# An mLSTM layer in fp32 on one core: five instead of four of eight chunks of the input projection by seven products

## The chip, the core and the metric

The program runs on one core of a Trainium2 chip. TensorE (PE) multiplies, VectorE (DVE), ScalarE (ACT) and GpSimd (POOL) work elementwise, SyncE (SP) issues DMAs. Each engine runs its own instructions in the order of the program and waits on semaphores for the others. The metric is the device time of one execution in microseconds; the kernel before has a median of 1795.51 us in three runs (1791.73 to 1797.22).

## The reference

One decoder layer of depth 1, so only the mLSTM mixer is computed, on 256 tokens of width 4096 in fp32, with 8 heads (query and key width 256, value width 512):

```python
h = rms_norm(x, norm_w)
u = h @ w_in                          # 4096 x 16400 columns
qk, v, og, z, ig, fg = split(u)
qk = silu(causal_dwconv(qk, conv_w, conv_b))      # 4 taps
# per head, in two chunks of 128 tokens:
a   = exp(decay - max) * (q @ k.T)                # causal
hc  = (a @ v + inter-chunk part) / max(|sum|, exp(-max))
hn  = hc * rsqrt(mean(hc * hc) + EPS) * out_norm_w
y   = hn * sigmoid(og) * silu(z)
out = x + y @ w_out                   # 4096 x 4096
```

## The kernel before

**Products.** Each fp32 operand is split into a high part (`hi`, rounded to the type fp32r) and the rest (`lo`). A product is three matmuls: hi by hi, hi by lo, lo by hi (`matmul3`, L138). The activations are the stationary side and stay in SBUF for a whole projection; the weights stream through as the moving side, 512 columns a matmul. `split` (L133) makes the two parts: ACT writes `hi` with a copy (L135), DVE writes `lo = src - hi` (L136). `operand` (L144) does this for a weight block of 128x1024, which is one buffer of the four `whi` and one of the four `wlo`; the raw block lies in one of six `wraw` buffers, loaded by SP with 512 KB a transfer (L157). All three kinds have the size of 1056 floats (RAW), 4224 bytes, so that the starts of neighbouring buffers differ by 33 times 128 bytes.

**Pairs and chunks.** The first phase projects head 0's q, k, v and the gates with plain products. Then 15 pairs of column blocks of `w_in` follow, 2 x 512 columns each: for head h first `qkv` (q and k; v), then `oz` (the output gate; z); head 0 has `oz` only. Four pairs of `w_out` (`o0` to `o3`) end the kernel. In `project_pair` (L317) the 4096 rows are 8 chunks of 512. A chunk in `FAST` (0, 2, 4, 6) is done by seven products of half blocks instead of eight (the Strassen-Winograd form): `STEPS` (L45) lists its loads, its four sums of weight blocks on DVE (`add`, L281) and its seven uses, named P1 to P7 after the PSUM bank they add into. Each use is one `operand` and 6 matmuls. A plain chunk is four uses of 12 matmuls each, without sums. The uses of a fast chunk form four groups, (P1), (P5, P3), (P7, P6, P2) and (P4), and after each group one use of a plain chunk follows.

**The rest of a head.** After a pair, `combine` (L349) reads the seven banks. What follows is put in a queue of small closures, of which `pump` runs some after every use: the four convolution taps of q and k (`taps`, L443) and their SiLU (`silu`, L451), the decay matrix, q k, row sums, values and a reciprocal root (`head`, L462, with `rsqrt`, L121), the gates (`gate_1`, L639), then `finish` and `turn`, which transposes y and writes it to DRAM (`spill`, by POOL). `build` (L196) makes the stationary operands of a chunk, `build_x` (L241) those of x after scaling. The order on each engine is fixed when the program is built.

**Names.** `w_qkv` is a raw block, `wh_qkv` and `wl_qkv` its parts, `..._P` those of a fast use; `w_qkv3_2_21` is head 3, chunk 2, block 21. `acc` and `pt` belong to the convolution, `sg` to the gate, `rs_...` and `ss` to the reciprocal root.

Of the kernel before, what the change touches and what calls it, by code (L numbers as in the profile page):

```python
# [716 lines left out]
```

## Time and profile before

| | us |
|---|---|
| median of 3 runs | 1795.51 |
| the profiled execution, its own time | 1793.31 |
| its span, first to last instruction | 1791.6 |
| PE busy | 1756.1 (98%) |
| DVE busy | 1655.5 (92%) |
| ACT busy | 1107.1 (62%) |

The profiled execution's time is 1.7 us over its span and 2.2 us under the median. A matmul or a DVE instruction is recorded longer than the distance to the next, since neighbours overlap in the pipeline; the distance between two starts is what an instruction costs when the engine has no gap. "Busy" counts overlapping time once.

### The profile page before, as it was taken

The page shows a single profiled execution, that of the slowest core. Times are in us where ns is not written, and L with a number is a line of the kernel's source. Part 1 is how long each engine was busy: PE and PEld are TensorE (multiplying, and loading weights), DVE is VectorE, ACT ScalarE, POOL GpSimd, SP SyncE. Part 2 cuts the span into 40 slices and gives each one's busy share as a digit, 9 for nine tenths or more (in the row PEclk, how much of TensorE's full clock was granted, in tenths as well). Part 3 has the DMA queues.
Part 4 walks back from the last instruction along what each step waited for, and adds up shares of the span by engine and source line. Part 5 has one row for each costly group of instructions (what it writes and reads, how often), then busy time and mean ns, then how long its engine had stood idle before and what let it go on. Part 6 is the DMA issues. An engine that isn't in the chain of part 4 may idle for free.

```text
span 1791.6 us, 21695 instructions
## 1 busy us (share of the span) xinstructions
PE 1756.1 (98%) x7804; PEld 1419.5 (79%) x7804; DVE 1655.5 (92%) x1823; ACT 1107.1 (62%) x1271; POOL 12.1 (1%) x29
## 2 busy tenths in 40 slices
PE   9979999999999999999999999999999989999998
PEld 8867878888888788788878887888788768787876
DVE  5899999999999999989998999899999999989897
ACT  7566666665666666656666566566656666565654
POOL 0000000000000000000000000000000000000000
PEclk9999999999999999999999999999999989999999
DMA  9755565556555656565556566655555747767563
GB/s 368 262 167 193 171 221 191 193 190 219 192 192 179 217 182 202 174 234 188 188 192 218 188 193 205 208 186 195 202 193 183 234 154 258 244 212 241 195 221 121
DMA packets 107724, 365.67 MB, mean 204 GB/s; under 512 B 12128, under 2 KB 12512, under 8 KB 107616
## 3 DMA queue, kind: packets, MB, share of 16 engines
q1 hardware_dynamic: 105360, 356.95, 59.4%
q0 software_dynamic: 1968, 6.82, 1.0%
q8 instruction: 61, 1.00, 0.2%
q10 hardware_dynamic: 288, 0.52, 0.1%
q14 instruction: 47, 0.39, 0.1%
HBM read 356.38 MB, written 7.86 MB: 203 GB/s over the span
## 4 chain that ended last, share of the span: by engine, by line
PE 86%; DVE 7%; ACT 3%; issue 2%; DMA 1%; SPq 0%; DVEq 0%; ACTq 0%
PE P_oz L140 11%; PE P_oz L141 11%; PE P_oz L142 11%; PE P_qkv L141 10%; PE P_qkv L142 10%; PE P_qkv L140 10%; PE P_o L141 5%; PE P_o L142 5%; PE P_o L140 5%; ACT wh_qkv_P L135 1%; PE first_P L140 1%; PE first_P L141 1%; PE first_P L142 1%; DVE wl_oz_P L136 1%; DVE wl_oz L136 1%
## 5 line engine op out<-in xcount | busy, mean ns | idle before, releaser
L135 ACT ACTIVATE wh_oz_P<-w_oz 128x1024 fp32r<-128x1024 f32 x224 | 233.8, 1056 | 166.2 <-DVE w_oz L281 85.7
L136 DVE TENSOR_TENSOR wl_oz_P<-w_oz,wh_oz_P 128x1024 fp32r<-128x1024 f32 x224 | 269.0, 1216 | 19.5 <-ACT wh_oz_P L135 19.5
L135 ACT ACTIVATE wh_qkv_P<-w_qkv 128x1024 fp32r<-128x1024 f32 x196 | 206.4, 1060 | 114.3 <-PE P_qkv L142 77.6
L136 DVE TENSOR_TENSOR wl_qkv_P<-w_qkv,wh_qkv_P 128x1024 fp32r<-128x1024 f32 x196 | 236.8, 1220 | 29.8 <-ACT wh_qkv_P L135 28.7
L141 PE MATMUL P_oz<-wl_oz,lhs_x 128*128 128x512 f32 x512 | 202.7, 396 | 0.0
L142 PE MATMUL P_oz<-wh_oz,lhs_x 128*128 128x512 f32 x512 | 201.3, 393 | 0.0
L140 PE MATMUL P_oz<-wh_oz,lhs_x 128*128 128x512 f32 x512 | 195.2, 396 | 1.8 <-ACT wh_oz L135 0.9
L141 PE MATMUL P_oz<-wl_oz_P,lhs_x 128*128 128x512 f32 x448 | 179.0, 400 | 1.1 <-DVE wl_oz_P L136 1.1
L140 PE MATMUL P_oz<-wh_oz_P,lhs_x 128*128 128x512 f32 x448 | 175.9, 402 | 3.9 <-ACT wh_oz_P L135 3.8
L141 PE MATMUL P_qkv<-wl_qkv,lhs_x 128*128 128x512 f32 x448 | 177.4, 396 | 0.9 <-DVE wl_qkv L136 0.9
L142 PE MATMUL P_oz<-wh_oz_P,lhs_x 128*128 128x512 f32 x448 | 177.1, 395 | 0.0
L142 PE MATMUL P_qkv<-wh_qkv,lhs_x 128*128 128x512 f32 x448 | 176.1, 393 | 0.0
L135 ACT ACTIVATE wh_o_P<-w_o 128x1024 fp32r<-128x1024 f32 x112 | 117.6, 1059 | 93.5 <-PE P_o L142 53.1
L135 ACT ACTIVATE wh_qkv<-w_qkv 128x1024 fp32r<-128x1024 f32 x112 | 118.5, 1058 | 79.2 <-PE P_qkv L142 66.0
L140 PE MATMUL P_qkv<-wh_qkv,lhs_x 128*128 128x512 f32 x448 | 166.7, 393 | 0.0
L135 ACT ACTIVATE wh_oz<-w_oz 128x1024 fp32r<-128x1024 f32 x128 | 134.8, 1053 | 47.4 <-PE P_oz L142 22.5
L136 DVE TENSOR_TENSOR wl_oz<-w_oz,wh_oz 128x1024 fp32r<-128x1024 f32 x128 | 155.7, 1217 | 7.5 <-ACT wh_oz L135 7.3
L281 DVE TENSOR_TENSOR w_oz<-w_oz,w_oz 128x1024 f32<-128x1024 f32 x128 | 155.7, 1217 | 0.5
L141 PE MATMUL P_qkv<-wl_qkv_P,lhs_x 128*128 128x512 f32 x392 | 154.7, 395 | 0.0
L142 PE MATMUL P_qkv<-wh_qkv_P,lhs_x 128*128 128x512 f32 x392 | 154.2, 393 | 0.0
L136 DVE TENSOR_TENSOR wl_o_P<-w_o,wh_o_P 128x1024 fp32r<-128x1024 f32 x112 | 135.3, 1219 | 18.9 <-ACT wh_o_P L135 18.8
L140 PE MATMUL P_qkv<-wh_qkv_P,lhs_x 128*128 128x512 f32 x392 | 150.2, 398 | 1.1 <-ACT wh_qkv_P L135 1.0
(216 smaller groups left out, 3436.7 us busy)
## 6 DMA issues: line engine op xcount, KB each, us to landing
w_oz<-in_w_in SPq DMA_DIRECT2D x256, 512.0 KB, 4.3
w_qkv<-in_w_in SPq DMA_DIRECT2D x224, 512.0 KB, 4.3
w_o<-in_w_out SPq DMA_DIRECT2D x128, 512.0 KB, 4.4
wf<-in_w_first SPq DMA_DIRECT2D x15, 528.0 KB, 6.7
wf<-in_w_first SPq DMA_DIRECT2D x15, 512.0 KB, 6.7
xr<-in_x SPq DMA_DIRECT2D x8, 512.0 KB, 8.6
xn<-in_xT SPq DMA_DIRECT2D x8, 512.0 KB, 5.7
xo<-in_x SPq DMA_DIRECT2D x16, 256.0 KB, 5.2
```

The costliest lines, as they stand in the source:

```text
L135: nc.scalar.activation(hi, src, AF.Copy)
L136: nc.vector.tensor_sub(lo, src, hi.bitcast(F32))
L140: nc.tensor.matmul(ps, a[0], b[0], start=first, stop=False)
L141: nc.tensor.matmul(ps, a[0], b[1], start=False, stop=False)
L142: nc.tensor.matmul(ps, a[1], b[0], start=False, stop=last)
L281: nc.vector.tensor_add(raw[step[1]], raw[step[1]], raw[step[2]])
```

## The change

Chunk 1 of `w_in` joins the fast chunks, so that a pair of `w_in` has five fast and three plain chunks; `w_out` keeps four and four. The plain uses are spread evenly over the 20 groups, so that 8 of the 20 have none behind them. `whi` and `wlo` shrink to 1024 floats (4096 bytes), and all eight buffers then start at the same place modulo 4096 bytes; the wide blocks of the first phase go through two pairs of other buffers. Some DVE work becomes other work: a tap is two ACT copies and one DVE addition for both halves, SiLU is ACT's own function in place of a sigmoid and a DVE product, `build_x` scales by the norm's weights on ACT, and ten of the twelve small steps of the reciprocal root of a head go to POOL, in another form of 13 steps there. The DMA scratch shrinks to 2048 bytes.

```diff
-FAST = (0, 2, 4, 6)
+FAST = {"x": (0, 1, 2, 4, 6), "y": (0, 2, 4, 6)}
...
-    def rsqrt(dst, src, n, tag):
+    def rsqrt(dst, src, n, tag, eng=nc.vector):
...
         nc.vector.tensor_scalar(r.bitcast(I32), i, -1.0, float(0x5F3759DF), op0=OP.mult, op1=OP.add)
         for it in range(3):
-            nc.vector.tensor_mul(t, r, r)
-            nc.vector.scalar_tensor_tensor(t, t, -0.5, src, op0=OP.mult, op1=OP.mult)
-            nc.vector.scalar_tensor_tensor(dst if it == 2 else r, t, 1.5, r, op0=OP.add, op1=OP.mult)
+            eng.tensor_mul(t, r, r)
+            eng.tensor_mul(t, t, src)
+            eng.tensor_scalar(t, t, -0.5, 1.5, op0=OP.mult, op1=OP.add)
+            eng.tensor_mul(dst if it == 2 else r, t, r)
...
-        hi = wpool.tile([P, RAW], F32R, name=f"wh_{name}", tag="whi")[:, :n]
-        lo = wpool.tile([P, RAW], F32R, name=f"wl_{name}", tag="wlo")[:, :n]
+        hi = wpool.tile([P, HK * NB], F32R, name=f"wh_{name}", tag="whi")[:, :n]
+        lo = wpool.tile([P, HK * NB], F32R, name=f"wl_{name}", tag="wlo")[:, :n]
         split(hi, lo, src)
         return hi, lo
 
+    def wide_operand(name, src, n):
+
+        tags = (("v0", "v1"), ("cA", "cB"))[n % 2]
+        hi, lo = (work.tile([P, RAW], F32R, name=f"w{i}_{name}", tag=tag)[:, :src.shape[-1]]
+                  for i, tag in enumerate(tags))
+        split(hi, lo, src)
+        return hi, lo
...
-        def scaled(j0):
-            def run():
-                if j0 == 0:
-                    nc.sync.dma_start(src, xT[:, c * CK:(c + 1) * CK, :])
-                for j in range(j0, j0 + 2):
-                    k = c * CK + j
-                    nc.vector.scalar_tensor_tensor(src[:, j, :], src[:, j, :], nw[:, k:k + 1], rstdB,
-                                                   op0=OP.mult, op1=OP.mult)
+        def scaled():
+            nc.sync.dma_start(src, xT[:, c * CK:(c + 1) * CK, :])
+            for j in range(CK):
+                nc.scalar.activation(src[:, j, :], src[:, j, :], AF.Copy, scale=nw[:, c * CK + j:c * CK + j + 1])
+            nc.vector.tensor_mul(src, src, rstdB.unsqueeze(1).to_broadcast([P, CK, T]))
...
-        for c in FAST:
-            for group in fast_steps(name, w, off, c):
-                steps += group
-                if plain:
-                    steps.append(plain.pop(0))
+        for i, group in enumerate(groups):
+            steps += group + plain[i * len(plain) // len(groups):(i + 1) * len(plain) // len(groups)]
...
-            def taps(a):
+            def tap(j):
                 def run():
-                    acc, pt, ct = t_["acc"], t_["pt"], ct0 + a
-                    for j in range(1, CONV):
-                        nc.vector.scalar_tensor_tensor(acc[:, a, j:], pt[:, a, :T - j], cw[:, 3 - j, ct:ct + 1],
-                                                       acc[:, a, j:], op0=OP.mult, op1=OP.add)
+                    acc, tp, pt = t_["acc"], t_["tp"], t_["pt"]
+                    for a in range(2):
+                        nc.scalar.activation(tp[:, a, :T - j], pt[:, a, :T - j], AF.Copy,
+                                             scale=cw[:, 3 - j, ct0 + a:ct0 + a + 1])
+                    nc.vector.tensor_add(acc[:, :, j:], acc[:, :, j:], tp[:, :, :T - j])
                 return run
 
             def silu():
-                nc.scalar.activation(t_["sg"], t_["acc"], AF.Sigmoid)
-                nc.vector.tensor_mul(t_["acc"], t_["acc"], t_["sg"])
+                nc.scalar.activation(t_["acc"], t_["acc"], AF.Silu)
...
-            nc.vector.tensor_scalar(ss, ss, 1.0 / DV, EPS, op0=OP.mult, op1=OP.add)
-            rsqrt(s2, ss, NT, f"h{h}")
+            nc.gpsimd.tensor_scalar(ss, ss, 1.0 / DV, EPS, op0=OP.mult, op1=OP.add)
+            rsqrt(s2, ss, NT, f"h{h}", nc.gpsimd)
...
-                sg[0] = big("sg", [P, NT, NB])
                 nc.scalar.activation(A, A, AF.Sigmoid)
-                nc.scalar.activation(sg[0], B, AF.Sigmoid)
+                nc.scalar.activation(B, B, AF.Silu)
 
-            todo += [gate_1, lambda B=B, sg=sg: nc.vector.tensor_mul(B, B, sg[0]),
-                     lambda A=A, B=B: nc.vector.tensor_mul(B, B, A)]
+            todo += [gate_1, lambda A=A, B=B: nc.vector.tensor_mul(B, B, A)]
...
-    nc = bacc.Bacc("TRN2", target_bir_lowering=False, num_devices=1, dynamic_dma_scratch_size=4096)
+    nc = bacc.Bacc("TRN2", target_bir_lowering=False, num_devices=1, dynamic_dma_scratch_size=2048)
```

The first place to look at is DVE in the pair `qkv3` at chunk 2, from its last sum on. Before, the sum of block 21 (L281), a plain split (`3_2`), the split for P4:

```order
L136 TENSOR_TENSOR wl_qkv3_2_P6_5065<-w_qkv3_2_11_4959,wh_qkv3_2_P6_5064 128x1024
L136 TENSOR_TENSOR wl_qkv3_2_P2_5075<-w_qkv3_2_21_5062,wh_qkv3_2_P2_5074 128x1024
L281 TENSOR_TENSOR w_qkv3_2_21_5062<-w_qkv3_2_21_5062,w_qkv3_2_11_4959 128x1024
L136 TENSOR_TENSOR wl_qkv3_3_2_5088<-w_qkv3_3_2_5085,wh_qkv3_3_2_5087 128x1024
L136 TENSOR_TENSOR wl_qkv3_2_P4_5104<-w_qkv3_2_21_5062,wh_qkv3_2_P4_5103 128x1024
L136 TENSOR_TENSOR wl_qkv3_3_3_5116<-w_qkv3_3_3_5113,wh_qkv3_3_3_5115 128x1024
```

Now, on the same engine at the same chunk:

```order
L138 TENSOR_TENSOR wl_qkv3_2_P6_5231<-w_qkv3_2_11_5143,wh_qkv3_2_P6_5230 128x1024
L138 TENSOR_TENSOR wl_qkv3_2_P2_5241<-w_qkv3_2_21_5228,wh_qkv3_2_P2_5240 128x1024
L287 TENSOR_TENSOR w_qkv3_2_21_5228<-w_qkv3_2_21_5228,w_qkv3_2_11_5143 128x1024
L138 TENSOR_TENSOR wl_qkv3_2_P4_5252<-w_qkv3_2_21_5228,wh_qkv3_2_P4_5251 128x1024
L138 TENSOR_TENSOR wl_qkv3_5_2_5264<-w_qkv3_5_2_5261,wh_qkv3_5_2_5263 128x1024
```

The split for P4 needs `wh_qkv3_2_P4`, which ACT makes from the sum; the plain split that stood between the sum and it now stands behind it.

The second place is ACT at the gate of head 3, inside the pair `qkv4`. Before, one table load and two sigmoids:

```order
L135 ACTIVATE wh_qkv4_0_P2_6303<-w_qkv4_0_21_6289 128x1024
L135 ACTIVATE wh_qkv4_1_2_6320<-w_qkv4_1_2_6318 128x1024
L642 ACT_TABLE_LOAD
L642 ACTIVATE A_oz3_6186<-A_oz3_6186 128x1024
L643 ACTIVATE sg_6315<-B_oz3_6187 128x1024
L135 ACTIVATE wh_qkv4_0_P4_6338<-w_qkv4_0_21_6289 128x1024
```

Now, at the gate of the same head:

```order
L137 ACTIVATE wh_qkv4_0_P2_6383<-w_qkv4_0_21_6381 128x1024
L644 ACT_TABLE_LOAD
L644 ACTIVATE A_oz3_6297<-A_oz3_6297 128x1024
L645 ACT_TABLE_LOAD
L645 ACTIVATE B_oz3_6298<-B_oz3_6298 128x1024
L137 ACTIVATE wh_qkv4_0_P4_6408<-w_qkv4_0_21_6381 128x1024
```

A second table load has come between the sigmoid and the SiLU, and the next `hi` of a weight block stands behind both.

## Rows read from the trace of the kernel before

**Rows 1.** The page: busy time of each engine over the whole span.

```profile
PE 1756.1 (98%) x7804; PEld 1419.5 (79%) x7804; DVE 1655.5 (92%) x1823; ACT 1107.1 (62%) x1271; POOL 12.1 (1%) x29
```

**Rows 2.** Windows by stage: length, then PE, PEld, DVE, ACT, POOL busy, clock, DMA.

```profile
0.90:202.60 201.70, 187.31 (x973) 156.90 (x974) 173.14 (x256) 132.64 (x185) 1.39 (x6) 0.98 0.70 243
555.30:729.20 173.90, 173.73 (x766) 140.34 (x765) 163.38 (x175) 109.22 (x123) 0.53 (x1) 1.00 0.59 197
1332.50:1524.20 191.70, 183.78 (x766) 144.62 (x766) 185.17 (x220) 121.71 (x147) 0.00 (x0) 0.96 0.61 206
1524.20:1608.60 84.40, 83.78 (x361) 67.49 (x360) 77.20 (x72) 48.00 (x48) 2.17 (x4) 1.00 0.66 225
```

**Rows 3.** Timeline of DVE: start, duration, instruction; first split of qkv3 and of qkv4.

```profile
552.35 1.22 DVE L136 TENSOR_TENSOR wl_qkv_P<-w_qkv,wh_qkv_P 128x1024 fp32r<-128x1024 f32 x1
...
726.25 1.22 DVE L136 TENSOR_TENSOR wl_qkv_P<-w_qkv,wh_qkv_P 128x1024 fp32r<-128x1024 f32 x1
```

**Rows 4.** Timeline of PE: first and last of 12 matmuls, chunk 5 then 7 of qkv3.

```profile
602.38 0.62 PE L140 MATMUL P_qkv<-wh_qkv,lhs_x 128*128 128x512 f32 x2
...
604.95 0.39 PE L142 MATMUL P_qkv<-wh_qkv,lhs_x 128*128 128x512 f32 x1
...
623.16 0.63 PE L140 MATMUL P_qkv<-wh_qkv,lhs_x 128*128 128x512 f32 x2
...
625.68 0.39 PE L142 MATMUL P_qkv<-wh_qkv,lhs_x 128*128 128x512 f32 x1
```

**Rows 5.** Groups by line: names, shapes, count, busy us, mean ns, idle before.

```profile
L136 DVE TENSOR_TENSOR wl_oz_P<-w_oz,wh_oz_P 128x1024 fp32r<-128x1024 f32 x224 | 269.0, 1216 | 19.5 <-ACT wh_oz_P L135 19.5
...
L642 ACT ACT_TABLE_LOAD x8 | 10.3, 1283 | 0.1
...
L642 ACT ACTIVATE A_oz<-A_oz 128x1024 f32<-128x1024 f32 x8 | 8.5, 1063 | 0.1
...
L544 POOL DMA_DIRECT2D spill<-yT x7 | 3.9, 554 | 1276.6 <-ACT yT L541 1276.6
L129 DVE TENSOR_TENSOR rs_t_h<-rs_r_h 128x2 f32<-128x2 f32 x24 | 3.7, 154 | 0.2
...
L709 POOL MEMSET const-float32-1.0<- 128x1 f32 x1 | 0.1, 98 | 0.0
```

**Rows 6.** Timeline of DVE without gaps: splits, combines of 512, one tap.

```profile
646.62 1.21 DVE L136 TENSOR_TENSOR wl_oz<-w_oz,wh_oz 128x1024 fp32r<-128x1024 f32 x1
647.75 0.68 DVE L362 TENSOR_TENSOR r_qkv<-r_qkv,p_qkv 128x512 f32<-128x512 f32 x1
648.35 0.68 DVE L362 TENSOR_TENSOR B_qkv<-B_qkv,p_qkv 128x512 f32<-128x512 f32 x1
...
659.98 0.47 DVE L447 SCALAR_TENSOR_TENSOR acc<-pt,cw,acc 128x254 f32<-128x254 f32 x1
660.38 1.21 DVE L136 TENSOR_TENSOR wl_oz<-w_oz,wh_oz 128x1024 fp32r<-128x1024 f32 x1
```

**Rows 7.** Timeline, all engines: a sum, the hi part of P4, its lo part (oz3).

```profile
699.88 1.22 DVE L281 TENSOR_TENSOR w_oz<-w_oz,w_oz 128x1024 f32<-128x1024 f32 x1
...
701.21 1.06 ACT L135 ACTIVATE wh_oz_P<-w_oz 128x1024 fp32r<-128x1024 f32 x1 [2.51 <-DVE w_oz L281]
...
702.30 1.23 DVE L136 TENSOR_TENSOR wl_oz_P<-w_oz,wh_oz_P 128x1024 fp32r<-128x1024 f32 x1 [1.21 <-ACT wh_oz_P L135]
```

**Rows 8.** Windows of 10 us in which DVE is full; columns as in rows 2.

```profile
1440.00:1450.00 10.00, 8.76 (x28) 6.05 (x26) 10.00 (x18) 3.81 (x4) 0.00 (x0) 0.83 0.46 157
...
150.00:160.00 10.00, 9.89 (x46) 7.72 (x45) 9.96 (x13) 6.12 (x8) 0.00 (x0) 1.00 0.68 213
```

More of the change, by code (lines that the diff above doesn't have):

```diff
@@ L318, in project_pair @@
         ps = {}
-        plain = [u for c in range(NCH) if c not in FAST for u in plain_steps(name, w, off, c)]
+        fast = FAST[of]
+        plain = [u for c in range(NCH) if c not in fast for u in plain_steps(name, w, off, c)]
+        groups = [g for c in fast for g in fast_steps(name, w, off, c)]
         steps = []
-        for c in FAST:
-            for group in fast_steps(name, w, off, c):
-                steps += group
-                if plain:
-                    steps.append(plain.pop(0))
-        assert not plain
-        uses = {s: len(FAST) * HK for s in TAGS}
+        for i, group in enumerate(groups):
+            steps += group + plain[i * len(plain) // len(groups):(i + 1) * len(plain) // len(groups)]
+        uses = {s: len(fast) * HK for s in TAGS}
         for s in ("P2", "P3", "P4", "P5"):
-            uses[s] += (NCH - len(FAST)) * CK
+            uses[s] += (NCH - len(fast)) * CK
         seen = dict.fromkeys(TAGS, 0)
-        left = {c: 7 if c in FAST else 4 for c in range(NCH)}
+        left = {c: 7 if c in fast else 4 for c in range(NCH)}
         for n, (c, make, cost) in enumerate(steps):
@@ L441, in turned, with head @@
                                          scale=cw[:, 3, ct0 + a:ct0 + a + 1], bias=cb[:, ct0 + a:ct0 + a + 1])
-            def taps(a):
+            def tap(j):
                 def run():
-                    acc, pt, ct = t_["acc"], t_["pt"], ct0 + a
-                    for j in range(1, CONV):
-                        nc.vector.scalar_tensor_tensor(acc[:, a, j:], pt[:, a, :T - j], cw[:, 3 - j, ct:ct + 1],
-                                                       acc[:, a, j:], op0=OP.mult, op1=OP.add)
+                    acc, tp, pt = t_["acc"], t_["tp"], t_["pt"]
[3 more added lines that the diff above has]
+                    nc.vector.tensor_add(acc[:, :, j:], acc[:, :, j:], tp[:, :, :T - j])
                 return run
             def silu():
-                nc.scalar.activation(t_["sg"], t_["acc"], AF.Sigmoid)
-                nc.vector.tensor_mul(t_["acc"], t_["acc"], t_["sg"])
-            return [turned, taps(0), taps(1), silu, lambda: split(qk[i][0], qk[i][1], t_["acc"])]
+                nc.scalar.activation(t_["acc"], t_["acc"], AF.Silu)
+            return [turned, tap(1), tap(2), tap(3), silu, lambda: split(qk[i][0], qk[i][1], t_["acc"])]
         return one(0) + one(1)
-    V = [lhs_pool.tile([P, NT, DV], F32R, name=f"v{part}") for part in range(2)]
     y = {}
-    def head(h):
+    def head(h, V):
         qT, kT = qk
@@ L546, in turn @@
         if h == HEADS - 1:
-            out += lazy(lambda: build(h, yT[0], "y"), 4 if h in FAST else 2)
+            out += lazy(lambda: build(h, yT[0], "y"), 4 if h in FAST["y"] else 2)
         return out
@@ L561, in mlstm_layer @@
     FW = GQ + DQK + DV
+    wides = 0
     for c in range(NCH):
@@ L581, in mlstm_layer @@
                 for k in range(k0 + a, k0 + z):
[L582 to L586 removed]
+                    nc.scalar.activation(xraw[:, k, :], xraw[:, k, :], AF.Copy, scale=nw[:, c * CK + k:c * CK + k + 1])
+                split(xh[:, k0 + a:k0 + z, :], xl[:, k0 + a:k0 + z, :], xraw[:, k0 + a:k0 + z, :])
+                ops = [wide_operand(f"f_{c}_{k0}_{a}", ws[0], wides), operand(f"f_{c}_{k0}_{a}", ws[1])]
+                wides += 1
                 for k in range(n):
@@ L604, in mlstm_layer @@
                     part()
+    V = [work.tile([P, RAW], F32R, name=f"v{part}", tag=f"v{part}")[:, :NT * DV].rearrange("p (t c) -> p t c", t=NT)
+         for part in range(2)]
     u0 = work.tile([P, NT, NB], F32, name="u_0", tag="cA")
@@ L616, in mlstm_layer @@
                                        op0=OP.mult, op1=OP.subtract)
-    hs, finish = head(0)
+    hs, finish = head(0, V)
     for c in range(5, NCH):
@@ L632, in mlstm_layer @@
         if what == "qkv":
-            hs, finish = head(h)
+            hs, finish = head(h, V)
             todo += [lambda t=t, B=B: split(V[0][:, t, :], V[1][:, t, :], B[:, t, :]) for t in range(NT)]
@@ L701 @@
                                         .reshape(KT, P, -1).transpose(1, 0, 2)).reshape(-1),
-        "w_in": np.concatenate([blocks_of(w_in, s1, s2) for _, _, s1, s2 in block_pairs()]),
+        "w_in": np.concatenate([blocks_of(w_in, s1, s2, "x") for _, _, s1, s2 in block_pairs()]),
         "conv_w": np.ascontiguousarray(inputs["a_conv_w"][0].reshape(CONV, 2 * QK // P, P).transpose(2, 0, 1)),
@@ L706 @@
         "out_norm_w": np.ascontiguousarray(inputs["a_out_norm_w"][0].reshape(KT, P).T),
-        "w_out": np.concatenate([blocks_of(w_out, [(a, NB)], [(a + NB, NB)]) for a in range(0, D, 2 * NB)]),
+        "w_out": np.concatenate([blocks_of(w_out, [(a, NB)], [(a + NB, NB)], "y") for a in range(0, D, 2 * NB)]),
     }
-    nc = bacc.Bacc("TRN2", target_bir_lowering=False, num_devices=1, dynamic_dma_scratch_size=4096)
+    nc = bacc.Bacc("TRN2", target_bir_lowering=False, num_devices=1, dynamic_dma_scratch_size=2048)
     args = [nc.dram_tensor(f"in_{name}", a.shape, mybir.dt.from_np(a.dtype), kind="ExternalInput").ap()
```

26 lines of the change are left out of this document (10 added, 16 removed).

## The prediction

> **What bounds the kernel now.** I read the page first: PE is busy 98% of the span and DVE 92%, ACT 62% [rows 1]. Shares over the whole span hide which engine waits for which, so I cut the span by stage [rows 2]. One head (the pairs qkv3 and oz3) takes 173.90 us; PE is busy 173.73 of them, DVE 163.38. The same length comes from DVE's first split of qkv3 to its first of qkv4, 726.25 - 552.35 [rows 3]. So PE bounds the heads and DVE has 10.5 us to spare in each. In the stage of oz7 and o0 (191.70 us), where the operands of `w_out` are built, it is the other way round: DVE is busy 185.17, PE 183.78. In o1 PE is busy 83.78 of 84.40. The first stage with oz0 (201.70) is full on neither, but DVE has 173.14 in it.
>
> Next come the prices. Twelve matmuls of a plain use start 0.234 us apart in one case, (604.95 - 602.38)/11, and 0.229 in another, (625.68 - 623.16)/11 [rows 4]; I take 0.231 as the mean. A DVE instruction of 1024 is recorded with 1.216 us [rows 5], but where DVE is full the next one starts after 1.13 (647.75 - 646.62), one of 512 costs 0.60, a tap 0.40 [rows 6]. These distances are what counts for an engine without gaps. Last, the chain from a sum to the split of that sum: the sum starts at 699.88, ACT's `hi` at 701.21, DVE's `lo` at 702.30 [rows 7]. That is 2.42 us from start to start, of which the sum itself takes 1.13; 1.29 are a gap unless other work stands between the two in DVE's order.
>
> **Part 1, PE.** A fast chunk has 7 uses of 6 matmuls (42) where a plain one has 4 of 12 (48). So each pair of `w_in` loses 6 matmuls, a head 12: 12 x 0.231 = 2.8 us. Over 15 pairs it is 20.8 us.
>
> **Part 2, alignment.** The two cases of rows 4 differ by 4.6 ns a matmul. The slow one reads buffer 3 of `whi` and `wlo`, the fast one buffer 0. Buffers lie 33 x 128 bytes apart, so their starts are odd and even multiples of 128 in turn, buffers 0 and 2 odd (160640 is 1255 x 128). All new buffers start at odd ones (the first at 993 x 128). If that is the cause, half of the matmuls gain 4.6 ns, on the mean 2.3 ns: 1.7 us for the 708 of a head, 0.8 for a pair of `w_out`. If it is not, the gain is nothing, and by the other end the same is lost. I take the gain. PE then needs 173.9 - 2.8 - 1.7 = 169.4 us a head.
>
> **Part 3, DVE's work.** A fast chunk has 7 splits and 4 sums, a plain one 4 splits: 7 more instructions a pair, 14 a head, 14 x 1.13 = 15.8 us more. Relief in a head: 12 taps x 0.40 become 6 additions x 0.60 (4.8 to 3.6, -1.2); two SiLU products of 512 and one gate product of 1024 go (-1.2 and -1.1); ten small steps go, recorded with 0.154 each [rows 5], which cost 0.07 between long ones and 0.2 in a chain by themselves; I take 0.1 (-1.0). Together -4.5. What DVE needs before lies between the sum of distances, 159 (120 x 1.13 for weights, 23 for the rest), and its busy time 163.4, which also holds the uncovered ends before gaps; I take 160, near the sum, since a fuller engine has fewer gaps. After: 160 + 15.8 - 4.5 = 171.3 us a head. That is already more than PE's 169.4.
>
> **Part 4, new gaps.** With 8 of 20 groups having no plain use behind them, less stands between a sum and its split; the order of the changed program shows how much. In a head, three splits for P4 stand directly behind their sum (1.29 each, 3.9), three have one instruction of 512 between (1.29 - 0.60 = 0.69, 2.1), twelve splits have one of 1024 between (0.16, 1.9): 7.9 us. Before, the same count gives 2.5, and PE's 10.5 us of cover hid it. Now it lies on the engine that has no cover: 171.3 + 7.9 = 179.2 us. DVE runs in order, so this doesn't shrink by PE's being early.
>
> **Part 5, other waits of a full DVE.** At the gate ACT now has sigmoid, a second table load and SiLU between DVE's last step on A and its product: 1.06 + 1.28 + 1.06 and two handovers of about 0.1 are 3.6 [rows 5, 7], against 2.9 of DVE work in between (0.60 + 2 x 1.13): 0.7. Taps, k's split and row sums also pass from DVE over ACT or PE back to DVE. Each has one to four instructions of 1.13 as cover, so between 0 and a gap like the 1.29 of rows 7; for all of them together I take 1.1. A head then takes 179.2 + 1.8 = 181.0, which is 7.1 more than now. ACT gets 6 splits x 1.06, 12 tap copies of at most 0.6 and a table load, some 15 us, on its 109 [rows 2]: 124 of 181, so it is no bound; its copies are hidden beside DVE's work, and where they are not, the 1.1 holds it. POOL's 13 steps lie between the row statistics and `finish`, which stands some 40 instructions later in DVE's order (about 40 us); even at the 0.554 of POOL's dearest row they are 7.2 us [rows 5], so `finish` doesn't wait. Weight transfers shift with their buffers; the DMA share is 0.59 [rows 2], and I cost them at nothing, inside the range.
>
> **The sum.** Six whole heads (qkv1 to oz6): 6 x 7.1 = 42.6; if Part 5 is nothing and DVE needs 159 before, 6 x 4.2 = 25; if Part 5 is three times larger and weight transfers arrive late by 1 us in each pair, 6 x 13 = 78. The pair qkv7: +3 (2 to 5). oz7 with o0, DVE-bound already: 7.9 of work for oz7's fifth chunk, -4.5 of relief, and 2 of new gaps, +5 (3 to 9). First phase with oz0: +7.9, +1 for the larger operands of chunk 1, -4.5 or less of a head's relief, -3.0 for 32 small splits of x that become 16 of 512 or less, -3.6 for `build_x` (32 x 0.40 to 8 x 1.13); that is near +1, but early in this stage DVE waits for ACT and DMA, so that some of the relief buys nothing: +4 (-4 to +12). o1 to o3 are PE-bound: 3 x -0.8 = -2.4 (0 at the other end). Together 42.6 + 3 + 5 + 4 - 2.4 = +52 us. On the profiled execution's 1793.3 (span 1791.6 and 1.7 around it) this is 1845; on the median, 2.2 higher, 1847. I forecast 1847 us, slower by 2.9%.
>
> **Rivals.**
>
> *PE stays the bound: faster.* If DVE could do its larger load within 169.4 us a head, the time falls by 20.8 and by 2.3 ns for each of 6750 matmuls (15.5), to 1759. For it: PE has no idle time today and DVE has 10.5 a head. Against it: the sum of Part 3 without any gap is 171.3. It decides at 169.4; DVE would need 2 us less than its instructions cost where it is full in rows 6.
>
> *DVE is the bound, but its gaps are filled.* Then a head takes 171.3, 2.6 less than now: 6 x -2.6 - 1 + 3 + 2 - 2.4 = -14, 1781. For it: before, DVE runs without a gap from 150 to 160 us [rows 8]. Against it: there, other work stood between sum and split, while in the changed order three splits a head stand directly behind.
>
> *The full DVE costs more.* Two mechanisms. POOL's steps may hold DVE up: 13 a head at 0.1 (the smallest row of POOL) to 0.55 (its dearest) [rows 5] are 1.3 to 7.2 us; at 3 us a head, 25 us more, 1872. And PE's clock may fall when PE waits: where DVE was full and PE busy 8.8 of 10 us, the granted clock was 0.83, a part at 1.2 instead of 2.4 GHz; where PE was busy 9.9 it was 1.00 [rows 8]. PE would be at 169 of 181, between the two. Each such window costs PE 1.7 us; its 11 us of slack a head cover six of them, so that the price comes only beyond.
>
> The Trainium skill speaks to the first of these: "SBUF — State Buffer", section "Who interferes with whom", says that a DVE instruction with two inputs in SBUF and a GpSimd instruction that reads SBUF exclude each other, and that the later one waits to the end of the earlier. No row here shows POOL computing beside DVE. By that rule the mechanism is certain and only its size is open, so that the 1872 would be the likelier end.
>
> **Chances.** The forecast (1818 to 1862): 66%. The costlier full DVE (above that): 23%. PE stays the bound: 4%. Gaps filled: 4%. Something in between that ends within 0.3% (5.4 us, about what a measurement of this kernel can tell from no change): 3%. So slower 0.89, same 0.03, faster 0.08. The low end of the range is the sum of the low ends, 25 + 2 + 3 - 4 - 2.4 = +24, 1819; the high end 78 + 5 + 9 + 12 = +104 would be 1899, and I cut it at 1890; some 15% are left out.
>
> **What would show it.** In the changed kernel's trace, windows over one head should show DVE busy at 94 to 97%, its idle time in gaps at P4 and P5, and PE below 98%, with waits of PE on `lo` parts of fast uses and on `hi` of P4; today it has next to none. The distance between DVE's first splits of two qkv pairs should be 179 to 184 us. At P4 of chunk 2 there should be a gap of 1.2 to 1.3 us behind the sum. Splits should still take 1.216, and matmuls of all plain uses 0.229 apart; 0.234 in any buffer would show Part 2 wrong. I am wrong if a head takes less than 175 us: then either DVE's instructions became cheaper or the gaps were hidden, and the waits of PE tell which.

## The result and the profile after

The changed kernel takes 1882.63 us (median of four runs, 1881.64 to 1883.72) where the kernel before takes 1795.09 (1791.73 to 1797.22): a ratio of 1.049, 95% interval 1.0471 to 1.0508. The forecast was 1847 with a range of 1818 to 1890. The direction and the bound are right, the loss is 87.5 us instead of 52. The time lies above 1862, where the prediction's own forecast ends, in the stretch that it left to the costlier full DVE (23%).

The page's first line, which answers to [rows 1]: PE goes from 98% to 94%, POOL from 12 to 115 us, DVE works 76.5 us more in all but keeps its share.

```profile
PE 1759.8 (94%) x7714; PEld 1405.0 (75%) x7714; DVE 1732.0 (92%) x1743; ACT 1203.4 (64%) x1469; POOL 114.7 (6%) x133
```

Windows by stage, columns as in [rows 2]: a head (qkv4 and oz4), then oz7 with o0, then o1.

```profile
769.00:953.70 184.70, 173.90 (x755) 137.99 (x754) 174.34 (x170) 118.76 (x142) 14.85 (x14) 0.99 0.54 185
...
1416.50:1620.70 204.20, 182.02 (x761) 139.25 (x760) 191.21 (x209) 131.73 (x164) 12.02 (x13) 0.98 0.58 197
1620.70:1704.00 83.30, 82.53 (x362) 67.44 (x361) 77.09 (x72) 48.03 (x49) 2.22 (x4) 1.00 0.67 227
```

In the head neither engine is full: PE is idle for 10.8 us, DVE for 10.4, so the busy shares don't say which one sets the pace. DVE's first splits of qkv4 and of qkv5 are 952.54 - 767.83 = 184.71 apart, where [rows 3] has 173.90. Added up from one start to the next, DVE's instructions of this head cost 170.9 us without gaps, more than the 169.4 that PE was to need; the other 13.8 are gaps between them, small ones of 0.1 among them that the busy time doesn't show. That DVE sets the pace is shown further down, by runs that change its order or its work (`e4_p4`, `e3_norelief`).

```profile
767.83 1.22 DVE L138 TENSOR_TENSOR wl_qkv_P<-w_qkv,wh_qkv_P 128x1024 fp32r<-128x1024 f32 x1
...
952.54 1.22 DVE L138 TENSOR_TENSOR wl_qkv_P<-w_qkv,wh_qkv_P 128x1024 fp32r<-128x1024 f32 x1
```

Where the 90.4 us of the span went (1882.0 - 1791.6), by the first matmuls of the pairs in both traces:

| stage | before, us | after, us | difference | forecast |
|---|---|---|---|---|
| first phase with oz0 | 209.2 | 212.0 | +2.8 | +4 |
| six heads, mean of one | 173.62 | 185.56 | 6 x 11.94 = +71.7 | +42.6 |
| qkv7 | 84.9 | 91.1 | +6.2 | +3 |
| oz7 and o0 | 191.7 | 204.2 | +12.5 | +5 |
| o1 to the end | 264.1 | 261.3 | -2.8 | -2.4 |

The gaps in detail. First the P4 of chunk 2 of qkv4, as in [rows 7]: the sum on DVE, ACT's `hi`, DVE's `lo`, which starts 2.43 us after its sum.

```profile
821.25 1.23 DVE L287 TENSOR_TENSOR w_qkv<-w_qkv,w_qkv 128x1024 f32<-128x1024 f32 x1
...
822.59 1.06 ACT L137 ACTIVATE wh_qkv_P<-w_qkv 128x1024 fp32r<-128x1024 f32 x1 [3.67 <-DVE w_qkv L287]
...
823.68 1.23 DVE L138 TENSOR_TENSOR wl_qkv_P<-w_qkv,wh_qkv_P 128x1024 fp32r<-128x1024 f32 x1 [1.21 <-ACT wh_qkv_P L137]
```

Then the gate of oz3. A table load stands before each of ACT's two functions, and the product on DVE stands behind all four steps.

```profile
779.75 0.69 DVE L366 TENSOR_TENSOR A_oz<-P_oz,r_oz 128x512 f32<-128x512 f32 x1
...
780.95 2.35 DVE L138 TENSOR_TENSOR wl_qkv_P<-w_qkv,wh_qkv_P 128x1024 fp32r<-128x1024 f32 x2
785.60 1.23 DVE L647 TENSOR_TENSOR B_oz<-B_oz,A_oz 128x1024 f32<-128x1024 f32 x1 [2.29 <-ACT B_oz L645]
...
780.84 1.28 ACT L644 ACT_TABLE_LOAD   x1
782.13 1.06 ACT L644 ACTIVATE A_oz<-A_oz 128x1024 f32<-128x1024 f32 x1
783.21 1.28 ACT L645 ACT_TABLE_LOAD   x1
784.51 1.06 ACT L645 ACTIVATE B_oz<-B_oz 128x1024 f32<-128x1024 f32 x1
```

Last, a gap that the prediction has no term for. In the same head PE waits 3.9 us in one piece, for the transposes of y behind `finish` (L522), which stands behind the gate's product on DVE. This is the longest of PE's waits there (us in total, times, longest):

```profile
PE py L540 <- DVE y L522: 3.9, 1, 3.9
```

The next use would not have started before 789.18 either. It is P4 of chunk 0, whose sum, too, stands on DVE right behind the gate's product; ACT starts its `hi` at 788.07:

```profile
788.67 0.43 PE L540 MATMUL py<-ident,y 128*128 128x128 f32 x1 [3.85 <-DVE y L522]
789.18 0.79 PE L142 MATMUL P_qkv<-wh_qkv_P,lhs_x 128*128 128x512 f32 x1
...
788.07 1.06 ACT L137 ACTIVATE wh_qkv_P<-w_qkv 128x1024 fp32r<-128x1024 f32 x1 [2.51 <-DVE w_qkv L287]
```

After the stop ACT has to wait for PE to free the `whi` buffers that P6 and P2 take, and DVE for ACT:

```profile
799.95 1.07 ACT L137 ACTIVATE wh_qkv_P<-w_qkv 128x1024 fp32r<-128x1024 f32 x1 [1.19 <-PE P_qkv L144]
801.53 1.06 ACT L137 ACTIVATE wh_qkv_P<-w_qkv 128x1024 fp32r<-128x1024 f32 x1 [0.52 <-PE P_qkv L144]
...
801.04 1.23 DVE L138 TENSOR_TENSOR wl_qkv_P<-w_qkv,wh_qkv_P 128x1024 fp32r<-128x1024 f32 x1 [0.25 <-ACT wh_qkv_P L137]
802.63 1.23 DVE L138 TENSOR_TENSOR wl_qkv_P<-w_qkv,wh_qkv_P 128x1024 fp32r<-128x1024 f32 x1 [0.36 <-ACT wh_qkv_P L137]
```

The groups by line give the prices: a split costs what it did in [rows 5], and POOL's small steps are recorded with about twice what I had taken as their upper bound (0.554).

```profile
L138 DVE TENSOR_TENSOR wl_oz_P<-w_oz,wh_oz_P 128x1024 fp32r<-128x1024 f32 x280 | 334.8, 1218 | 24.2 <-ACT wh_oz_P L137 23.4
...
L130 POOL TENSOR_TENSOR rs_t_h<-rs_r_h 128x2 f32<-128x2 f32 x24 | 25.2, 1050 | 23.9 <-DVE rs_r_h L128 22.6
...
L517 POOL TENSOR_SCALAR ss<-ss 128x2 f32<-128x2 f32 x8 | 10.6, 1321 | 1086.2 <-ACT y L513 1086.2
```

### The profile page after: what moved, and what is told of

The parts are those of the page before. It is cut to its first block, busy times and chain, and to the rows that moved or that the text cites. A ratio compares the mean times of both kernels' runs of the same rounds, so it can differ in the third digit from the quotient of the medians.

```text
span 1882.0 us, 21814 instructions
## 1 busy us (share of the span) xinstructions
PE 1759.8 (94%) x7714; PEld 1405.0 (75%) x7714; DVE 1732.0 (92%) x1743; ACT 1203.4 (64%) x1469; POOL 114.7 (6%) x133
## 4 chain that ended last, share of the span: by engine, by line
PE 40%; DVE 26%; issue 20%; ACT 9%; DMA 3%; POOL 1%; SPq 0%; ACTq 0%; DVEq 0%; POOLq 0%
PE P_oz L143 6%; PE P_oz L142 6%; PE P_oz L144 6%; DVE w_qkv L287 5%; PE P_qkv L142 5%; PE P_qkv L143 4%; PE P_qkv L144 4%; DVE wl_oz_P L138 4%; DVE w_oz L287 4%; DVE wl_qkv_P L138 4%; ACT wh_qkv_P L137 2%; PE P_o L142 2%; PE P_o L143 2%; PE P_o L144 2%; DVE wl_qkv L138 2%
## 5 line engine op out<-in xcount | busy, mean ns | idle before, releaser
L137 ACT ACTIVATE wh_oz_P<-w_oz 128x1024 fp32r<-128x1024 f32 x280 | 287.5, 1053 | 142.9 <-DVE w_oz L287 117.9
L138 DVE TENSOR_TENSOR wl_oz_P<-w_oz,wh_oz_P 128x1024 fp32r<-128x1024 f32 x280 | 334.8, 1218 | 24.2 <-ACT wh_oz_P L137 23.4
L138 DVE TENSOR_TENSOR wl_qkv_P<-w_qkv,wh_qkv_P 128x1024 fp32r<-128x1024 f32 x245 | 291.5, 1219 | 29.5 <-ACT wh_qkv_P L137 28.5
L142 PE MATMUL P_oz<-wh_oz_P,lhs_x 128*128 128x512 f32 x560 | 216.8, 403 | 27.4 <-ACT wh_oz_P L137 27.1
L144 PE MATMUL P_oz<-wh_oz_P,lhs_x 128*128 128x512 f32 x560 | 220.5, 394 | 0.0
L142 PE MATMUL P_qkv<-wh_qkv_P,lhs_x 128*128 128x512 f32 x490 | 190.5, 402 | 3.2 <-ACT wh_qkv_P L137 1.9
L144 PE MATMUL P_qkv<-wh_qkv_P,lhs_x 128*128 128x512 f32 x490 | 193.2, 394 | 0.0
L287 DVE TENSOR_TENSOR w_qkv<-w_qkv,w_qkv 128x1024 f32<-128x1024 f32 x140 | 170.9, 1221 | 1.9
L142 PE MATMUL P_oz<-wh_oz,lhs_x 128*128 128x512 f32 x384 | 144.9, 400 | 6.7 <-ACT wh_oz L137 6.7
L142 PEld LDWEIGHTS P_oz<-wh_oz_P,lhs_x 128*128 128x128 f32 x560 | 104.6, 190 | 60.8 <-ACT wh_oz_P L137 39.4
L144 PE MATMUL P_oz<-wh_oz,lhs_x 128*128 128x512 f32 x384 | 149.9, 390 | 0.0
L143 PEld LDWEIGHTS P_oz<-wl_oz_P,lhs_x 128*128 128x128 f32 x560 | 106.3, 190 | 49.3 <-DVE wl_oz_P L138 27.3
L144 PE MATMUL P_qkv<-wh_qkv,lhs_x 128*128 128x512 f32 x336 | 131.5, 391 | 0.0
L142 PE MATMUL P_qkv<-wh_qkv,lhs_x 128*128 128x512 f32 x336 | 129.5, 407 | 0.5
```

Source lines behind the costliest of these rows:

```text
L137: nc.scalar.activation(hi, src, AF.Copy)
L138: nc.vector.tensor_sub(lo, src, hi.bitcast(F32))
L142: nc.tensor.matmul(ps, a[0], b[0], start=first, stop=False)
L143: nc.tensor.matmul(ps, a[0], b[1], start=False, stop=False)
L144: nc.tensor.matmul(ps, a[1], b[0], start=False, stop=last)
L287: nc.vector.tensor_add(raw[step[1]], raw[step[1]], raw[step[2]])
```

## The experiments

Theory: the fifth chunk puts more on DVE than a head's time of PE holds, and DVE's gaps add to it; alignment and relief help. Rivals: the relief's own handovers to ACT and POOL are the loss; POOL holds DVE up; the gaps move instead of going. Ratios are to the kernel before, with 95% intervals; "a head" is the mean of six.

**Four chunks again** (`e1_four`).

```
-FAST = {"x": (0, 1, 2, 4, 6), "y": (0, 2, 4, 6)}
+FAST = {"x": (0, 2, 4, 6), "y": (0, 2, 4, 6)}
```

> The changed kernel with four fast chunks of w_in again; its relief of VectorE and its buffers of one alignment stay. Theory (the fifth chunk makes VectorE the bound, everything else helps): TensorE bounds the heads again, a head takes 171 to 172.5 us (173.6 less the gain of alignment of 1.7 to 2.4), the total is 1776 us (1766 to 1785), PE busy 98% or more. Rival (the relief itself, by its handovers to ACT and POOL, is what slows the changed kernel): 1850 us or more. Rival (alignment buys nothing): a head of 173.6 us, total 1790 to 1800.

1772.03 us, ratio 0.987 (0.9856 to 0.9883): faster than both kernels (1.3% faster than the one before). A head takes 172.2 us, and its window (qkv4 and oz4) shows PE back at 171.0 of 171.7 and DVE with 12.9 to spare:

```profile
721.80:893.50 171.70, 170.98 (x767) 140.46 (x766) 158.76 (x156) 115.38 (x136) 11.76 (x14) 1.00 0.61 199
```

So the fifth chunk alone costs 1882.6 - 1772.0 = 110.6 us, and the rest of the change is worth 23.1. That the handovers are the loss is refuted: they are all still in this kernel.

**Alignment alone, both ways** (`e2_odd`, `e2_even`), in the kernel before.

```
-        hi = wpool.tile([P, RAW], F32R, name=f"wh_{name}", tag="whi")[:, :n]
-        lo = wpool.tile([P, RAW], F32R, name=f"wl_{name}", tag="wlo")[:, :n]
+        hi = wpool.tile([P, RAW + 32], F32R, name=f"wh_{name}", tag="whi")[:, :n]
+        lo = wpool.tile([P, RAW + 32], F32R, name=f"wl_{name}", tag="wlo")[:, :n]
```

and in the even one also, ahead of `wpool`,

```
+    padpool = ctx.enter_context(tc.tile_pool(name="padpool", bufs=1))
+    padt = padpool.tile([P, 32], F32, name="padt")
```

> The kernel before with whi and wlo buffers of 1088 instead of 1056 numbers, so that all eight start at odd multiples of 128 bytes; nothing else changes. Theory (odd multiples make the matmul that reads them faster): plain matmuls 0.228 to 0.230 us apart in all buffers, the mean falling from 0.231 by 1.3 to 3.3 ns, a head of 171.2 to 172.9 us, the total 1773 to 1786 us. Rival (the place of the buffer has no part in it): no change, 1790 to 1798 us.

> The kernel before with whi and wlo buffers of 1088 numbers behind a pad of 128 bytes, so that all eight start at even multiples of 128 bytes. Theory (even multiples are the slow ones): matmuls 0.232 to 0.234 us apart in all buffers, the total 1797 to 1812 us. Rival (what counts is that all buffers lie alike, not where): as fast as with odd multiples, 1773 to 1786 us.

Odd: 1776.31 us, ratio 0.9893 (0.9879 to 0.9906). Even: 1802.52, ratio 1.004 (1.0027 to 1.0054). First and last of the 12 matmuls of a plain use of qkv3, in the odd kernel 226.4 ns apart, (611.05 - 608.56)/11:

```profile
608.56 0.62 PE L140 MATMUL P_qkv<-wh_qkv,lhs_x 128*128 128x512 f32 x2
...
611.05 0.39 PE L142 MATMUL P_qkv<-wh_qkv,lhs_x 128*128 128x512 f32 x1
```

and in the even one 232.7, (619.92 - 617.36)/11:

```profile
617.36 0.64 PE L142 MATMUL P_qkv<-wh_qkv,lhs_x 128*128 128x512 f32 x2
...
619.92 0.39 PE L144 MATMUL P_qkv<-wh_qkv,lhs_x 128*128 128x512 f32 x1
```

Over all matmuls of 512 columns that follow each other at once the means are 227.3 ns (odd), 231.0 (before, mixed) and 232.6 (even). The place decides, not that all lie alike. In the changed kernel the mean is 227.7.

**Relief undone** (`e3_norelief`), with five chunks: taps, SiLU and gate products and the reciprocal root as in the kernel before.

```
+                        nc.vector.scalar_tensor_tensor(acc[:, a, j:], pt[:, a, :T - j], cw[:, 3 - j, ct:ct + 1],
+                                                       acc[:, a, j:], op0=OP.mult, op1=OP.add)
...
+                nc.scalar.activation(t_["tp"], t_["acc"], AF.Sigmoid)
+                nc.vector.tensor_mul(t_["acc"], t_["acc"], t_["tp"])
...
+            rsqrt(s2, ss, NT, f"h{h}")
...
+            todo += [gate_1, lambda B=B, sg=sg: nc.vector.tensor_mul(B, B, sg[0]),
+                     lambda A=A, B=B: nc.vector.tensor_mul(B, B, A)]
```

> The changed kernel with the relief of a head undone: taps, SiLU and gate products and the small steps of the reciprocal root are VectorE's again; five fast chunks and the buffers stay. Theory (relief is worth its instructions, 4.5 us of VectorE a head, less the gate's gap of 2.4 that goes): a head of 187 to 191 us against 185.5, the total 1895 to 1920 us. Rival (the handovers to ACT and POOL cost as much as the relief saves): 1870 to 1890 us.

1901.37 us, ratio 1.0596 (1.0577 to 1.0614); a head 187.6. In the head of qkv4 DVE's instructions cost 175.1 instead of 170.9, so the 4.5 us of relief were priced well (4.2), but a head is only 2.0 longer, since gaps went the other way. The relief helps, by 19 us in all, as the theory had it.

**The order at P4** (`e4_p4`).

```
-         ("use", "12", "P7"), ("load", "21"), ("use", "11", "P6"), ("use", "21", "P2"), ("add", "21", "11"), ("gap",),
+         ("load", "21"), ("use", "21", "P2"), ("add", "21", "11"), ("use", "12", "P7"), ("use", "11", "P6"), ("gap",),
```

> The changed kernel with the third group of a fast chunk in another order: P2 and the sum for P4 come first, then P7 and P6, so that two splits stand between that sum and P4's split. Theory (the three gaps of 1.29 us a head at P4 add to the time of a full VectorE): a head falls from 185.5 by 3.9 to 181.6 us, the total by 7 x 3.9 = 27 to 1855 us (1848 to 1864). Rival (the gaps were idle time that something else, ACT or TensorE, sets anyway and it comes back at other places): 1875 to 1890 us, with as much idle time on VectorE as before the edit.

1834.14 us, ratio 1.0217 (1.0201 to 1.0232), 48 less than the changed kernel where I expected 27, and below the expected 1848 to 1864. A head takes 179.1. DVE's instructions cost the same 170.9 and the gaps fall from 13.8 to 8.5, but not as I had asked for: the built order still puts the sum behind P6, so two of the gaps of 1.29 stay. P4 has 3.3 us of gaps instead of 6.1, P6 and P2 0.1 instead of 1.4, a new gap of 1.75 stands at P5 of chunk 1, and the gate's gap shrinks to 0.71, as DVE has one more instruction in front of the product:

```profile
758.25 0.69 DVE L366 TENSOR_TENSOR A_oz<-P_oz,r_oz 128x512 f32<-128x512 f32 x1
...
760.59 1.22 DVE L287 TENSOR_TENSOR w_qkv<-w_qkv,w_qkv 128x1024 f32<-128x1024 f32 x1
762.43 1.23 DVE L647 TENSOR_TENSOR B_oz<-B_oz,A_oz 128x1024 f32<-128x1024 f32 x1 [0.63 <-ACT B_oz L645]
```

**The order at P4, wholly** (`e9_order`): P2 and the sum go into the second group.

```
+         ("load", "22"), ("add", "12", "22"), ("use", "11", "P5"), ("add", "11", "22"),
+         ("load", "21"), ("use", "21", "P2"), ("add", "21", "11"), ("use", "22", "P3"), ("gap",),
+         ("use", "12", "P7"), ("use", "11", "P6"), ("gap",),
...
```

> The changed kernel with P2 and the sum for P4 moved into the second group, between P5 and P3, so that in VectorE's order two or more instructions of 1024 stand between that sum and P4's split; all sums stay on VectorE. Theory (VectorE's instructions cost 170.9 us a head and the rest of 185.5 is gaps that the order makes): without the gaps at P4 (6.1 us a head) and at P6 and P2 (1.4) a head takes 175 to 179 us, the total 1805 to 1835 us. Rival (gaps taken away at P4 come back at other places, as with the gate): 1850 to 1885 us.

1835.23 us, ratio 1.0218 (1.02 to 1.0236), just above the expected 1805 to 1835; a head 179.5, half a us above what I expected. The gaps at P4 are gone but for 0.4 us: here the sum and the three splits behind it, P4's last, follow without a gap.

```profile
798.89 1.22 DVE L288 TENSOR_TENSOR w_qkv<-w_qkv,w_qkv 128x1024 f32<-128x1024 f32 x1
800.02 3.49 DVE L139 TENSOR_TENSOR wl_qkv_P<-w_qkv,wh_qkv_P 128x1024 fp32r<-128x1024 f32 x3
```

The gaps still make 8.5 us: the gate's 2.38 is back, sums that change their operand in place take 0.12 each 13 times, and plain splits got gaps of 0.2 to 1.0. So the order can give back some 6 us a head; part of each gain returns elsewhere.

**The gate** (`e5_gate`): two sigmoids and two products, as before the change.

```
-                nc.scalar.activation(B, B, AF.Silu)
+                nc.scalar.activation(sg[0], B, AF.Sigmoid)
...
+            todo += [gate_1, lambda B=B, sg=sg: nc.vector.tensor_mul(B, B, sg[0]),
+                     lambda A=A, B=B: nc.vector.tensor_mul(B, B, A)]
```

> The changed kernel with the gate as before: two sigmoids on ACT without a second table load, and two products on VectorE. Theory (the gate's wait of 2.4 us a head is a cost of the change): one instruction of 1024 more, 1.13, less 2.4, so 1.2 us less a head, the total 1872 us (1866 to 1879). Rival (the wait is idle time that comes back elsewhere, the product alone counts): 1884 to 1894 us.

1884.72 us, ratio 1.05 (1.0485 to 1.0515): 2.1 more than the changed kernel, which the two intervals don't tell apart. The theory fell, and the time is at the lower end of the rival's range. The gate's gap did shrink, from 2.29 idle to 0.87:

```profile
785.77 1.23 DVE L650 TENSOR_TENSOR B_oz<-B_oz,sg 128x1024 f32<-128x1024 f32 x1 [0.87 <-ACT sg L648]
```

but the order behind it changed too, and P4's gaps in oz4 grew; the gaps of the head are 15.0 us instead of 13.8. A gap that is removed by itself does not say what is won.

**POOL's small steps** (`e6_pool`): the reciprocal root of a head on DVE again.

```
-            rsqrt(s2, ss, NT, f"h{h}", nc.gpsimd)
+            rsqrt(s2, ss, NT, f"h{h}")
...
```

> The changed kernel with the steps of the reciprocal root of a head on VectorE again (8 or 10 short steps a head) and none on POOL. Theory (POOL waits for VectorE and doesn't hold it up): 0.1 to 0.2 us for each step comes back on VectorE, 8 heads of 1 to 2 us, the total 1887 to 1900 us. Rival (POOL's 13 steps hold a full VectorE up, by 1.3 to 7.2 us a head as the prediction bounded it): 1830 to 1880 us.

1881.84 us, ratio 1.0484 (1.0469 to 1.0498): the same as the changed kernel, and outside both expectations. DVE's instructions cost 0.7 us more in the head of qkv4 (171.6), its gaps 0.5 less. POOL's steps neither save nor cost anything that can be measured. In the changed kernel's trace the 97 DVE instructions of 1024 that run beside one of them are recorded with 1.220 us on the mean, the 1188 others with 1.219.

**P4's sum on POOL** (`e8_poolsum`, and `e9_poolsum` in the order of `e9_order`).

```
+                    eng = nc.gpsimd if step[1] == "21" else nc.vector
+                    eng.tensor_add(raw[step[1]], raw[step[1]], raw[step[2]])
```

> The changed kernel with the sum for P4 (one of four sums of a fast chunk, 128x1024) on POOL. Theory (POOL and VectorE do not hinder each other, as the distance of VectorE's splits of 1.137 us beside POOL's small steps against 1.136 without suggests): VectorE loses 10 x 1.13 = 11.3 us a head and the gaps at P4, a head takes 170 to 176 us, the total 1780 to 1815 us. Rival (the two exclude each other, so that VectorE stands for as long as POOL's sum runs, 1.1 us or more): a head of 184 us or more, the total 1875 to 1960 us, and longer splits or distances on VectorE beside POOL's sums.

1972.62 us, ratio 1.099 (1.0975 to 1.1006), more than the rival's upper end. POOL takes 2.4 us and more for the sum, and P4's split, directly behind, waits for it and for `hi`:

```profile
865.82 1.22 DVE L138 TENSOR_TENSOR wl_qkv_P<-w_qkv,wh_qkv_P 128x1024 fp32r<-128x1024 f32 x1 [3.65 <-ACT wh_qkv_P L137]
...
862.30 2.39 POOL L288 TENSOR_TENSOR w_qkv<-w_qkv,w_qkv 128x1024 f32<-128x1024 f32 x1 [15.14 <-DVE wl_qkv_P L138]
```

Here DVE was mostly waiting while POOL ran. Still 24 splits, each beside a sum, last over 1.5 us, up to 3.43. The next run shows more of it.

> The same order, and the sum for P4 on POOL, with three splits of VectorE (3.4 us) between P2's split and P4's. Theory (POOL's sum takes 2.4 to 3.2 us, does not hold VectorE up, and was only waited for where P4 stood directly behind): VectorE needs 159.6 us a head and a few of gaps, TensorE bounds the heads at 169 to 171 us, the total 1757 us (1743 to 1775). Rival (the sum on POOL is late for P4 here too, by 1 us or more each): a head of 174 us or more, 1790 to 1840 us.

1922.05 us, ratio 1.0715 (1.0693 to 1.0738); a head 190.4. The theory fell. A split of DVE that stands beside POOL's sum is recorded with 3.41 us instead of 1.22:

```profile
858.70 3.41 DVE L139 TENSOR_TENSOR wl_qkv<-w_qkv,wh_qkv 128x1024 fp32r<-128x1024 f32 x1
862.03 2.35 DVE L139 TENSOR_TENSOR wl_qkv_P<-w_qkv,wh_qkv_P 128x1024 fp32r<-128x1024 f32 x2
...
857.87 3.15 POOL L289 TENSOR_TENSOR w_qkv<-w_qkv,w_qkv 128x1024 f32<-128x1024 f32 x1 [10.82 <-DVE w_qkv L289]
```

67 of 1019 splits last over 1.5 us, each of them beside a sum on POOL; together they are 133 us longer than 67 x 1.22. In the changed kernel there is none. POOL's sums stretch as well, to 3.98 us on the mean in the oz pairs. The lines above fit an exclusion: POOL's sum ends at 861.02, and the split that started at 858.70 ends 1.09 later.

**The gate's product on POOL as well** (`e10_gatepool`).

```
+            todo += [gate_1, lambda A=A, B=B: nc.gpsimd.tensor_mul(B, B, A), lambda: None, lambda: None]
```

> As the kernel with P4's sum on POOL in the new order, and the gate's product of 1024 on POOL too. Theory (TensorE bounds the heads by then): within 6 us of that kernel. Rival (VectorE still bounds, by the gate's wait of 2.4 and the product of 1.13): 15 to 28 us less than that kernel.

1935.84 us, ratio 1.0784 (1.0768 to 1.08): 14 more than `e9_poolsum`. Neither expectation held; both had taken POOL's work as free.

**The best of it** (`e11_four_p4`): four chunks with the order of `e4_p4`.

> Four fast chunks of w_in with the relief and the new buffers, and P2 with the sum for P4 at the head of the third group (the order that took 48 us off with five chunks). Theory (heads are bound by TensorE with four chunks, so gaps of VectorE count only in oz0, oz7 and o0): heads of 171.5 to 172 us as without the order, 1 to 7 us less in the other stages, the total 1768 us (1763 to 1772). Rival (TensorE feels the order of uses in the heads too): a change of more than 1 us a head either way, 1755 or 1785 us.

1761.62 us, ratio 0.9815 (0.9801 to 0.9828), below the expected 1763 to 1772. The heads gain only 0.6 each (171.6), the first of them being the longest; the last five take 170.5, and PE is busy in every part of them (the window is rounded up):

```profile
720.10:890.70 170.60, 170.60 (x767) 140.49 (x767) 158.57 (x156) 115.66 (x136) 10.84 (x14) 1.00 0.60 201
```

The pairs qkv7 to o0 give 3.6 together, the end 1.7, the first phase with oz0 1.5. PE is the bound where the heads settle, and yet it waited 0.7 a head in `e1_four`: the order mattered there too.

## Why the prediction was right, and where its sizes were off

**What bounds, Part 1, Part 3: right.** DVE becomes the bound of the heads. Its instructions without gaps cost 170.9 us in the head of qkv4, 171.3 were forecast; `e3_norelief` confirms the relief's share (4.2 against 4.5). With four chunks PE is the bound again (`e1_four`), so the loss is the fifth chunk's. Of the signs that were named, the distance between first splits, 184.71, is just above 179 to 184; the others came as forecast: DVE busy at 94%, PE at 94%, 1.29 at P4 of chunk 2, splits of 1.218. Weight transfers were costed at nothing, and no wait of PE, DVE or ACT in that head is put down to a DMA.

**Part 2: right in mechanism and sign, low in size.** Odd starts are the fast ones (`e2_odd`, `e2_even`). I took 2.3 ns a matmul from the two kinds of buffer in [rows 4]; measured are 3.7 (231.0 to 227.3), because the odd buffers, too, are faster in a kernel that has no even ones: 227.3 instead of 229.8. Why is not shown. That is worth 18.8 us by itself where PE bounds. In the changed kernel it buys little, since PE waits.

**Part 4: right, 7.8 us against 7.9.** Three P4 of 1.29 and three of 0.61 to 0.67, as worked out, and all twelve of 0.16: two at P4 (0.16 and 0.14), which makes 6.1 us there; three at P6 (0.16 and 0.16, and one inside a longer wait); seven at P5, which stands behind two sums. There the split starts 2.40 to 2.64 us after the first sum, where two instructions cost 2.27, but most of the gap shows as a late second sum (0.12) and little as a wait of the split (0.03 at five of them), 1.2 us together:

```profile
793.74 2.48 DVE L287 TENSOR_TENSOR w_qkv<-w_qkv,w_qkv 128x1024 f32<-128x1024 f32 x2
796.16 1.23 DVE L138 TENSOR_TENSOR wl_qkv_P<-w_qkv,wh_qkv_P 128x1024 fp32r<-128x1024 f32 x1
```

**Part 5 is the step that failed in size: 1.8 us forecast, 6.0 measured.** Three terms make most of it in that head.
- The gate: 0.7 forecast, 2.38 measured. I counted one table load between A and the product; there are two, and sigmoid's stands behind A as well: 1.28 + 1.06 + 1.28 + 1.06 from 780.84 to 785.57. A is ready at 780.44, but ACT is at two `hi` copies until 780.82.
- Sums that change an operand which the instruction just before them on DVE reads or writes start 0.12 later than others, 15 times: 1.7 us. Seven of these are the late second sums at P5 and lie within Part 4's 0.16; the other eight, 0.9 us, had no term. The rule holds without exception in the trace: all 136 such sums start 0.115 to 0.116 late, the 228 others at most 0.04. It was in the trace of before, too (10 times in the same head, 1.2 us), hidden as PE was the bound.
- The ring DVE, PE, ACT, DVE: PE stops for 3.9 us, and behind it `hi` parts of P6 and P2 wait for buffers that PE still reads: 0.77 us in two places, and 0.33 in a third like them 140 us later, 0.9 in all without the 0.16 of Part 4 in it. I had let PE's 11 us of slack a head cover its own lateness. With four buffers of `whi`, PE's delay comes back to DVE before that slack is used up. The gate's gap alone doesn't start this ring: in `e9_order` it is the same 2.37, and no wait of PE in that head is over 1.0. In `e5_gate` it is 0.87, and PE still stops for 2.95, for the `hi` of P4, whose sum stands right behind the gate's first product as it does in the changed kernel; `e9_order` has moved that sum. No run moves that one sum alone.

```profile
789.36 0.51 PE L142 MATMUL P_qkv<-wh_qkv_P,lhs_x 128*128 128x512 f32 x1 [2.95 <-ACT wh_qkv_P L137]
```

- The other 1.8 us are small waits, none over 0.35.

7.8 + 6.0 are the 13.8 of gaps, where 9.7 were forecast; the mean head is another 0.8 longer than this one, and before it was 0.3 shorter than the one used. Gaps also explain qkv7 (+6.2 against +3): DVE's instructions cost about 83 of its 91.1 us, the other 8 are gaps, where the forecast left room for 5. In oz7 with o0 DVE's work grew by 6.0 us (185.17 to 191.21) and its idle time by 6.5 (6.5 to 13.0), against 3.4 and 2 in the sum. Of the 2.6 by which the work was short, 1.1 is one instruction of 1024 more that falls into the later window; the gaps were short by 4.5, as in the heads.

**The rivals.** PE as the bound fell for five chunks. Gaps filled (1781) fell too, even with the best order tried: 1834. The costlier full DVE came nearest in time (1872). The forecast's own stretch, 1818 to 1862, was missed; that the time still lies in the range is due to its width and not to the sum. Of the rival's two mechanisms POOL's fell: its steps are recorded with 1.05 us each on the mean of L130 instead of at most 0.554, yet DVE loses nothing by them (`e6_pool`). PE's clock seems to have had a small part. Behind PE's stop of 3.9 us the granted clock falls towards the lower of its two levels (1.2 of 2.4 GHz), to 0.78 from 790 to 795 us and, behind the same stop in the next head, to 0.51 from 975 to 980; columns as in [rows 2]:

```profile
790.00:795.00 5.00, 5.00 (x20) 4.10 (x19) 4.97 (x6) 2.70 (x5) 0.00 (x0) 0.78 0.79 260
975.00:980.00 5.00, 5.00 (x14) 3.94 (x13) 4.97 (x6) 2.62 (x5) 0.00 (x0) 0.51 0.73 247
```

That next head takes 186.8 us, and the three waits behind its stop are 0.81, 0.92 and 0.45 us where the head of qkv4 has 0.33 and 0.44, so 1.4 more. Over the six heads the granted clock is 0.97 to 0.99; in the same head of `e9_order`, which has no such stop, it is 1.00. No run changes the clock alone.

The Trainium skill's rule that the two engines exclude each other ("SBUF — State Buffer", "Who interferes with whom") is borne out by `e9_poolsum` (3.41 against 1.22), for instructions of 1024; the small steps hold DVE up too little to be seen, so the rule decides nothing about this change.

What stays open: why the gaps that are left in `e9_order` (8.5 us) come back when others go. The order of the instructions is built anew with each edit, and no run here holds it fixed while one gap is removed.

## What to carry to other kernels

A trade that takes 2.8 us from one engine and gives 15.8 to another is decided by the receiver's own sum, gaps included: add up its starts, then every place where it waits for another engine's answer to its own last instruction. Count the whole ring for such a wait, with each table load and the few buffers that tie a late engine back to the full one. Parts of a change can pull apart: alignment and relief were worth 23 us with four chunks (alignment alone 18.8), the fifth chunk lost 111, and without it the kernel is faster than both.
